# Gates of the last 64 dense tokens are read from the stage buffers instead of from DRAM

## The chip, the cores and the metric

One core of one Trainium2 chip runs the whole kernel. The metric is the device time of one execution in microseconds, given as the median of several runs. The engines are TensorE (PE; its weight loads are PEld), VectorE (DVE), ScalarE (ACT), GpSimd (POOL) and SyncE (SP), which here only issues transfers.

## What is computed

The kernel computes one encoder block on 512 tokens of width 1024: adaLN, two attention branches, a merged projection, and a PEER layer. Only the PEER layer matters here. It has 16384 experts, each one row of `expert_u` and one of `expert_v`; every token picks 16 experts in each of 8 heads, 128 in all, each with a gate.

```python
cand = (v1[..., :, None] + v2[..., None, :])      # scores of pairs of sub-keys
top, ci = lax.top_k(cand, PEER_TOPK)              # 16 experts a head
eidx = e1 * PEER_N_KEYS + e2                      # expert number, e1 and e2 below 128
gate = jax.nn.softmax(top, axis=-1)
act = jax.nn.gelu(jnp.einsum('td,thkd->thk', xc, expert_u[eidx]), approximate=False)
wts = gate * act
y = jnp.einsum('thk,thkd->td', wts, expert_v[eidx])
```

## The kernel before

The 512 tokens lie as four blocks of 128. Block 0 is done sparsely: for each of its 128 slots the chosen rows are gathered by GpSimd (`gather`, L1056), and VectorE makes a dot product (`dot`, L1062) or adds a weighted row to `acc` (`add`, L1071). These `jobs` are strewn over the rest of the kernel by `run_jobs`: `J0` = 48 of them in the gate stage, the others in the main loop.

Blocks 1 to 3, the 384 dense tokens, are done against all experts, 128 experts at a time. Expert group `e` (0 to 127) has three steps. First the activation: `gelu_s` (L872) multiplies `uT[e]` with all dense tokens in 24 matmuls and leaves 128 x 384 values `am`. For `e` below 96, `run_ahead` (L881) does this early and parks the result in DRAM (`gls`); for the others it is done inside the main loop. Second the product with the gates. Third the accumulation `y += (gated am)^T @ v[e]`, 18 matmuls of 128x512 (L1220), with the operands split into a high and a low half by `split` (L90: ScalarE makes the high half at L91, VectorE the low half at L92). `w4` loads a weight block into `raw` (L799) and gives the tiles for its halves, `whi` and `wlo`.

The gates come from a stage of their own (L1092 to L1150), which turns the sparse choice into a dense table of gates. For each dense block `slots` (L1021) gives expert numbers and gates. Then four tokens at a time VectorE builds one-hot tiles `oh` (L1125) and `og` (L1130), TensorE multiplies them into PSUM (`pg`, L1137), and ScalarE copies the result into `stage` (L1139). A `stage` tile holds 128 x 128 expert numbers by 32 tokens; there are two of them in turn. When 32 tokens (a group) are full, SyncE writes the tile to DRAM in four pieces, one for each quarter of the experts (`gd`, L1146). There are 12 groups, 96 copies and 48 writes.

The main loop (L1196 to L1223) reads the gates back. `stage_s` (L1161) loads, for every eighth expert group, a tile `gch` with the gates of eight expert groups and all 12 token groups (L1164, 1.5 MB), and the values `am`; it runs four expert groups ahead. The first expert groups in the order are 96 to 103. L1201 then multiplies `am` by `gch`, and ScalarE and VectorE split the product into `ah` and `al`. `py`, the accumulators, take the PSUM banks of the gate stage.

Each engine and each transfer queue works through its instructions in order; the order is chosen when the program is built, by a planner that estimates when each instruction could run, so that loads and jobs can stand earlier than in the text. Tiles of a closed pool give up their place; a tile that is put there waits, tile by tile, for the last use of what was there. The pool of the main loop (`lp`, L1158) is opened after those of the gate stage (`gt`) and of the selection (`sel`) are closed.

## Time and profile before

| what | us |
|---|---|
| runs | 2009.19, 2010.34, 2011.33 |
| median | 2010.34 |
| the profiled execution | 2011.68 |
| its span, first to last instruction | 2009.8 |
| TensorE busy in the span | 1873.7 |
| VectorE busy | 1593.2 |
| ScalarE busy | 842.7 |
| GpSimd busy | 698.0 |

[...] The gate stage's copies run from 938.7 to 1314.3 us of the span, the main loop from there to the end. An average over the span hides which engine sets the pace in which stage. So it is read together with views of single stretches: the timeline (instructions in order of time, with the idle time before each and what ended it), the chain of work that ended last, and busy times by stretch. Busy times of TensorE are those of pipelined instructions with modelled ends.

### The profile page before, as it was taken

Reading aid. Unit: us, or ns where it says so; the run is one execution under the profiler, and the core shown is the slowest. Engines: PE = TensorE matmul, PEld = TensorE weight load, DVE = VectorE, ACT = ScalarE, POOL = GpSimd, SP = SyncE. Lnnn points to the kernel's source line nnn. Section 1 sums busy time; section 2 is a strip of 40 time slices with the busy share of each in tenths; the row PEclk is TensorE's granted clock in tenths of the full one; section 3 lists DMA queues with packets and bytes.
Section 4 is the critical chain, followed back from the end, with each engine's and each line's share of the span. In section 5 each row is a group of like instructions: output and inputs, shape, how many; then the busy total and the mean of one; then the engine's idle time right before and its main releaser. Section 6 shows DMA issues by size and latency. Waiting matters only on the chain.

```text
span 2009.8 us, 28332 instructions
## 1 busy us (share of the span) xinstructions
PE 1873.7 (93%) x9858; PEld 1620.1 (81%) x9858; DVE 1593.2 (79%) x3276; ACT 842.7 (42%) x1330; POOL 698.0 (35%) x534
## 2 busy tenths in 40 slices
PE   6999998989899899999989999839999999999998
PEld 5987777778677788899989999828888888878886
DVE  7488585886775759999979989968778888888764
ACT  3444454645633333345545555513333333333342
POOL 2554332352235522012444147233234334323200
PEclk9999999999999999999999999969999999999999
DMA  7334242122256322468688979889999999999962
GB/s 262 86 120 121 63 145 60 35 87 84 59 152 215 128 72 81 147 226 276 229 295 316 322 274 322 299 287 371 360 320 354 342 354 330 355 361 325 345 225 93
DMA packets 206417, 447.30 MB, mean 223 GB/s; under 512 B 17297, under 2 KB 104642, under 8 KB 206146
## 3 DMA queue, kind: packets, MB, share of 16 engines
q1 hardware_dynamic: 168592, 309.14, 45.5%
q0 software_dynamic: 36864, 134.23, 18.8%
q10 hardware_dynamic: 818, 2.12, 0.3%
q8 instruction: 77, 1.26, 0.3%
q14 instruction: 66, 0.54, 0.1%
HBM read 397.20 MB, written 48.23 MB: 222 GB/s over the span
## 4 chain that ended last, share of the span: by engine, by line
PE 51%; DVE 16%; DMA 6%; issue 3%; ACT 2%; POOL 1%; SPq 0%; DVEq 0%; ACTq 0%; POOLq 0%
PE y L1220 26%; PE pj L86 7%; PE pj L87 7%; PE pj L88 7%; DMA raw<-uT 3%; DVE wlo L92 2%; DVE og L1130 2%; PE pg L1137 1%; DVE mr L933 1%; DMA raw<-w_ada 1%; DVE idx L935 1%; ACT whi L91 1%; DMA raw<-expert_v 1%; DVE oh L1125 1%; DVE idx L932 1%
## 5 line engine op out<-in xcount | busy, mean ns | idle before, releaser
L91 ACT ACTIVATE whi<-raw 128x1024 fp32r<-128x1024 f32 (+3 forms) x431 | 382.0, 893 | 382.6 <-PE pj L88 108.5
L92 DVE TENSOR_TENSOR wlo<-raw,whi 128x1024 fp32r<-128x1024 f32 (+3 forms) x339 | 376.9, 1114 | 98.1 <-ACT whi L91 96.7
L86 PE MATMUL pj<-h2h,whi 128*128 128x384 f32 x1008 | 345.8, 343 | 12.0 <-ACT am L879 10.9
L88 PE MATMUL pj<-h2h,wlo 128*128 128x384 f32 x1008 | 344.8, 342 | 5.0 <-DVE wlo L92 5.0
L87 PE MATMUL pj<-h2l,whi 128*128 128x384 f32 x1008 | 345.3, 343 | 0.0
L1058 POOL DMA_INDIRECT gat<-expert_v,eidx x128 | 211.9, 1656 | 316.9 <-DVE acc L1076 219.2
L1058 POOL DMA_INDIRECT gat<-expert_u,eidx x128 | 169.1, 1321 | 401.9 <-DVE gscr L1064 228.2
L1220 PE MATMUL y<-whi,ah 128*128 128x512 f32 x768 | 232.5, 397 | 33.3 <-ACT ah L91 28.4
L1220 PE MATMUL y<-wlo,ah 128*128 128x512 f32 x768 | 243.3, 397 | 0.7 <-DVE wlo L92 0.7
L92 POOL TENSOR_TENSOR wlo<-raw,whi 128x512 fp32r<-128x512 f32 (+2 forms) x92 | 146.5, 1598 | 278.7 <-ACT whi L91 256.0
L1220 PE MATMUL y<-whi,al 128*128 128x512 f32 x768 | 234.5, 395 | 0.0
L91 ACT ACTIVATE ah<-am 128x384 fp32r<-128x384 f32 x128 | 67.0, 524 | 333.5 <-PE y L1220 229.2
L86 PEld LDWEIGHTS pj<-h2h,whi 128*128 128x128 f32 x1008 | 192.2, 191 | 15.7 <-ACT am L879 12.9
L86 PE MATMUL pj<-whi,hh 128*128 128x512 f32 (+2 forms) x512 | 191.7, 387 | 9.8 <-DVE gA L651 4.4
L1220 PEld LDWEIGHTS y<-whi,ah 128*128 128x128 f32 x768 | 144.3, 189 | 67.7 <-ACT ah L91 28.6
L87 PE MATMUL pj<-wlo,hh 128*128 128x512 f32 (+2 forms) x512 | 196.2, 384 | 2.3 <-DVE wlo L92 2.3
L88 PEld LDWEIGHTS pj<-h2h,wlo 128*128 128x128 f32 x1008 | 191.9, 190 | 6.3 <-DVE wlo L92 6.3
L87 PEld LDWEIGHTS pj<-h2l,whi 128*128 128x128 f32 x1008 | 191.8, 190 | 1.1
L88 PE MATMUL pj<-whi,hl 128*128 128x512 f32 (+2 forms) x512 | 191.1, 380 | 0.0
L1220 PEld LDWEIGHTS y<-wlo,ah 128*128 128x128 f32 x768 | 144.7, 188 | 36.1 <-DVE wlo L92 1.2
L1220 PEld LDWEIGHTS y<-whi,al 128*128 128x128 f32 x768 | 144.2, 188 | 35.3
L1076 DVE SCALAR_TENSOR_TENSOR acc<-gat,wts,acc 128x1024 f32<-128x1024 f32 x127 | 162.4, 1279 | 9.6 <-DMA gat<-expert_v,eidx 9.2
(313 smaller groups left out, 3209.5 us busy)
## 6 DMA issues: line engine op xcount, KB each, us to landing
raw<-uT SPq DMA_DIRECT2D x128, 512.0 KB
raw<-expert_v SPq DMA_DIRECT2D x128, 512.0 KB
gd<-stage SPq DMA_DIRECT2D x48, 512.0 KB
gch<-gd SPq DMA_DIRECT2D x16, 1536.0 KB
raw<-w_in SPq DMA_DIRECT2D x88, 256.0 KB
am<-gls SPq DMA_DIRECT2D x96, 192.0 KB
gls<-am SPq DMA_DIRECT2D x94, 192.0 KB
raw<-w_ada SPq DMA_DIRECT2D x64, 256.0 KB
```

Source lines behind the costliest of these rows:

```text
L86: nc.tensor.matmul(ps, lh, rh, start=start, stop=False)
L87: nc.tensor.matmul(ps, lh, rl, start=False, stop=False)
L88: nc.tensor.matmul(ps, ll, rh, start=False, stop=stop)
L91: nc.scalar.activation(hi, raw, AF.Copy)
L92: (eng or nc.vector).tensor_tensor(lo, raw, hi.bitcast(F32), op=OP.subtract)
L932: nc.vector.max_index(out=i[:, 0:8], in_max=v[:, 0:8], in_values=s)
L933: nc.vector.match_replace(out=r, in_to_replace=v[:, 0:8], in_values=s, imm_value=-3.0e38)
L935: nc.vector.max_index(out=i[:, 8:16], in_max=v[:, 8:16], in_values=r)
L1058: nc.gpsimd.indirect_dma_start(out=t, out_offset=None, in_=src, in_offset=bass.IndirectOffsetOnAxis(ap=eidx[:, s:s + 1], axis=0))
L1076: nc.vector.scalar_tensor_tensor(acc, t, wts[:, s:s + 1], acc, op0=OP.mult, op1=OP.add)
L1130: nc.vector.tensor_tensor(o, oh[0].rearrange("p e t -> p t e"), gp[i][:, ts, None].to_broadcast([128, T, 128]), op=OP.mult)
L1220: nc.tensor.matmul(ys[b][n], l[:, bs], r[:, n * 512:n * 512 + 512], start=n_ == 0 and i == 0, stop=n_ == 127 and i == 2)
```

## The change

The two `stage` tiles become the two halves of one tile `stg` in the pool `g0`, which lives until the end of the kernel. Group `grp` (0 to 11) is built in half `grp % 2`, as before. Groups 0 to 9 are written to DRAM as before; groups 10 and 11 are not written, and their halves stay. The DRAM table and `gch` shrink from 12 to 10 token groups. The multiply by the gates becomes two: 320 values by `gch`, 64 values by `stg`. In the gate stage `slots` for block 0 now allocates its tiles ahead of `iota`.

```diff
-    RT, OB, SB, J0, GB = 8, 3, 2, 48, 4
+    RT, OB, J0, GB = 8, 3, 48, 4
...
+    stg = g0.tile([128, 2, 128, 32], F32, name="stage")
     gt = K.wk = Pool("gates")
...
+    e1, e2, g = slots(gt, 0)
     iota = gt.tile([128, 128, T], HF, name="iota")
     nc.vector.tensor_copy(iota, ioti[:, :, None].to_broadcast([128, 128, T]))
-    e1, e2, g = slots(gt, 0)
...
-            if tb == 0:
-                st = gt.tile([128, 128, 32], F32, name="stage", bufs=SB)
+            grp = 4 * b + t0 // 32
+            st = stg[:, grp % 2]
...
-            if tb == 28:
+            if tb == 28 and grp < 10:
                 for c in range(4):
-                    nc.sync.dma_start(gd[c][4 * b + t0 // 32].rearrange("c p e t -> p c (e t)"),
+                    nc.sync.dma_start(gd[c][grp].rearrange("c p e t -> p c (e t)"),
...
-            gch[e // 8] = lp.tile([128, 12, 8, 32], F32, name="gch", bufs=2)
+            gch[e // 8] = lp.tile([128, 10, 8, 32], F32, name="gch", bufs=2)
...
-        nc.vector.tensor_tensor(amv, amv, gch[e // 8][:, :, e % 8, :], op=OP.mult)
+        nc.vector.tensor_tensor(amv[:, :10], amv[:, :10], gch[e // 8][:, :, e % 8, :], op=OP.mult)
+        nc.vector.tensor_tensor(amv[:, 10:], amv[:, 10:], stg[:, :, e, :], op=OP.mult)
...
-        A['gd'] = [dram.tile([12, 4, 128, 8, 32], F32, name=f"gd{c}") for c in range(4)]
+        A['gd'] = [dram.tile([10, 4, 128, 8, 32], F32, name=f"gd{c}") for c in range(4)]
```

## Rows read from the trace of the kernel before

**Rows 1.** Page, first part: busy us, share of the span and instructions, each engine.
```profile
PE 1873.7 (93%) x9858; PEld 1620.1 (81%) x9858; DVE 1593.2 (79%) x3276; ACT 842.7 (42%) x1330; POOL 698.0 (35%) x534
```

**Rows 2.** Timeline, hand-over: start, us, engine, line, out<-in, count [idle before <-releaser].
```profile
1314.26 1.06 ACT L1139 ACTIVATE stage<-pg 128x512 f32<-128x512 f32 x1 [1.28 <-PE pg L1137]
...
1314.44 1.23 DVE L1064 SCALAR_TENSOR_TENSOR gscr<-gat,h2tok 128x1024 bf16<-128x1024 f32 x1
...
1315.35 3.82 SPq L1146 DMA_DIRECT2D gd<-stage  x4
...
1318.49 0.18 DVE L1069 TENSOR_TENSOR wts<-wts,gate 128x16 f32<-128x16 f32 x1 [0.28 <-ACT wts L1068]
...
1322.53 1.28 DVE L1076 SCALAR_TENSOR_TENSOR acc<-gat,wts,acc 128x1024 f32<-128x1024 f32 x1 [3.86 <-DMA gat<-expert_v,eidx]
...
1329.30 1.06 SPq L1164 DMA_DIRECT2D gch<-gd  x2
...
1341.39 1.96 DVE L1201 TENSOR_TENSOR am<-am,gch 128x384 f32<-128x384 f32 x4 [9.58 <-DMA gch<-gd]
...
1342.61 1.22 PE L1220 MATMUL y<-whi,ah 128*128 128x512 f32 x2 [28.38 <-ACT ah L91]
```

**Rows 3.** Chain that ended last, 1225 to 1372: start us, us, what.
```profile
1271.60 10.62 DMA raw<-uT
...
1317.40 11.76 DMA gd<-stage
1329.30 11.99 DMA gch<-gd
...
1357.24 4.20 PE y L1220 x18
```

**Rows 4.** Groups by line, 1342 to 2010: busy us, mean ns, idle before, releasers.
```profile
L1220 PE MATMUL y<-wlo,ah 128*128 128x512 f32 x768 | 243.3, 397 | 0.7 <-DVE wlo L92 0.7
...
L88 PE MATMUL pj<-h2h,wlo 128*128 128x384 f32 x208 | 71.3, 343 | 0.9 <-DVE wlo L92 0.9
...
L1201 DVE TENSOR_TENSOR am<-am,gch 128x384 f32<-128x384 f32 x127 | 69.6, 554 | 36.5 <-DMA am<-gls 27.2 <-ACT am L879 8.7
L91 ACT ACTIVATE ah<-am 128x384 fp32r<-128x384 f32 x128 | 67.0, 524 | 333.5 <-PE y L1220 229.2 <-issue 51.5 <-DVE am L1201 42.9
...
L1069 DVE TENSOR_TENSOR wts<-wts,gate 128x16 f32<-128x16 f32 x5 | 0.9, 178 | 0.6 <-ACT wts L1068 0.6
```

**Rows 5.** Busy by stretch: length; PE, PEld, DVE, ACT, POOL; PEclk, DMA share, GB/s.
```profile
1342.00:1366.00 24.00, 23.39 (x105) 20.45 (x106) 19.91 (x24) 8.51 (x13) 10.57 (x8) 0.91 0.69 233
...
1316.00:1342.00 26.00, 0.00 (x0) 0.00 (x0) 9.39 (x12) 0.22 (x1) 8.03 (x9) 0.50 1.02 358
1342.00:1900.00 558.00, 549.74 (x2489) 461.67 (x2490) 455.98 (x593) 192.24 (x265) 207.66 (x169) 0.99 0.95 343
1900.00:2003.00 103.00, 102.79 (x441) 82.38 (x439) 55.13 (x75) 34.45 (x46) 2.20 (x2) 1.00 0.53 171
```

**Rows 6.** Timeline of SyncE's queue, writes of the two groups before the last.
```profile
1262.53 3.21 SPq L1146 DMA_DIRECT2D gd<-stage  x4
...
1297.84 3.16 SPq L1146 DMA_DIRECT2D gd<-stage  x4
```

**Rows 7.** Groups by line and form, VectorE, whole span.
```profile
L952 DVE TENSOR_TENSOR cand<-vals 128x64 f32<-128x64 f32 x16 | 5.3, 334 | 0.0
```

**Rows 8.** Timeline, TensorE at the end of the gate stage.
```profile
1300.33 0.55 PE L1137 MATMUL pg<-og,oh 128*128 128x128 f16 x7 [0.35 <-DVE og L1130]
...
1303.00 0.91 PE L1137 MATMUL pg<-og,oh 128*128 128x128 f16 x7 [0.30 <-DVE og L1130]
```

**Rows 9.** One line, L1034: duration ns min/median/max, first and last start.
```profile
L1034 DVE TENSOR_TENSOR ef<-eq x4: 412/416/420, 883.5 to 1029.5; 128x256 f32<-128x256 bf16 x4
```

**Rows 10.** Timeline of the start: two pieces of one tile are read.
```profile
6.33 1.23 DVE L252 SCALAR_TENSOR_TENSOR sq<-xt 128x1024 bf16<-128x1024 f32 x1 [5.20 <-DMA xt<-x]
...
8.98 1.23 DVE L252 SCALAR_TENSOR_TENSOR sq<-xt 128x1024 bf16<-128x1024 f32 x1 [0.44 <-DMA xt<-x]
```

## The prediction

> **What bounds the kernel now.** I read the engine table of the page first: TensorE is busy for 93% of the span [rows 1], so the question is where it is not. The timeline of the hand-over from the gate stage to the main loop shows the largest hole after the start-up: TensorE stops when the last gate matmuls are done, and its first matmul of the main loop starts at 1342.61 after 28.38 us of idleness [rows 2]. The reader should follow that hole down the timeline. ScalarE copies the last four tokens' gates into `stage` at 1314.26 for 1.06 us. SyncE issues the four writes of the last group from 1315.35, and only at 1329.30 does it issue the first read back. VectorE's first multiply starts at 1341.39; ScalarE's split and TensorE at 1342.61 follow [rows 2]. The chain that ended last prices the two transfers: 11.76 us for the write that landed last and 11.99 us for the read [rows 3]. Together with the issue they are the hole; nothing else is late in it.

> The second question is whether time won there is kept until the end. The main loop after the hole is paced by TensorE. Its accumulations take 4.20 us for 18 matmuls, one expert after another [rows 3], and it is busy for 549.7 of 558 us and then for 102.8 of 103 [rows 5]: 8.5 us idle in the whole loop, 0.6 of them before its first matmul. So a loop that starts earlier ends earlier, as long as VectorE (456 of 558 us busy), the transfers (0.95 of the engines' time) and ScalarE (192 of 558) keep up [rows 5].

> **The change part by part.** *The round trip leaves the path.* The first chunk read will need only groups 0 to 9. Group 9 is the write issued at 1262.53, two before the last [rows 6]. With the last write's 11.76 us after 3.2 us of issue it has landed by about 1278, and a read like the present one (11.99 us) is in by about 1290, some 25 us before the last gates are copied at 1315.32. What must be free for it is the place of the `gch` buffer. By the code's sizes `sel` (6656 bytes a partition) and the `rb`, `sh`, `rkm`, `rkt` tiles of `slots` (3584) make 10240, exactly the new `gch`; the next 10240 are `eq` and `ef`. That the two pools start at the same address is my inference. The last use of `eq` and `ef` by VectorE begins at 1029.5 [rows 9], so both places would be long free; `iota`, which is read to the end, now lies behind them.

> *What is late next.* The multiply by groups 10 and 11 waits for the last copy, which ends at 1315.32. From the start of the first multiply to TensorE's start it is 1342.61 - 1341.39 = 1.22 us now [rows 2]; with a 64-wide multiply, about 0.33 us shorter, 0.89. The earliest start is thus 1316.2. But VectorE then has dot products of the sparse jobs, three from 1314.44 on, and a small product at 1318.49 behind them [rows 2]. They are queued work that goes on without the gates, and the multiply stands behind one to all of them: a start between 1316.6 and 1319.6. I take the middle, 1318.1, a gain of 1342.6 - 1318.1 = 24.5 us. The outer bound is a sum `acc` placed in front of it, which now ends at 1323.8 because it waits for its gather [rows 2]: start 1324.7, gain 17.9.

> *Clock.* [...] But the clock had fallen before the hole: seven gate matmuls take 0.55 us at 1300.33 and 0.91 at 1303.00, when TensorE runs only short bursts [rows 8]. [...]

> *One VectorE instruction more per expert.* The 384-wide multiply takes 554 ns, the 16-wide one of the same kind 178 [rows 4], so 1.02 ns an element: 320 wide 489, 64 wide 227. The sum of 716 is 162 ns more, 128 times, 21 us. The dearest row for 64 elements is the addition with repeated operands, 334 ns [rows 7]: then 269 ns more, 34 us. The cheap end is nothing, where VectorE was waiting anyway; a gain is excluded, since no element is saved. I take 21, as the 64-wide multiply is of the kind of [rows 4]. The work that hides it is VectorE's own waiting: 102 of 558 us while the jobs run, 48 of 103 after them [rows 5]. [...]

> *Jobs that move.* In the hole VectorE did 9.4 us of work and the transfer engines were full at 1.02 and 358 GB/s [rows 5]; those were 2.1 MB of gates out, 3.1 MB of gates in and eight gathers of 0.5 MB. The gathers and sums (9.4 us on VectorE) now fall into the loop. VectorE gets 21 + 9 = 30 us more against 102 us of waiting. The transfers get 4.2 MB more from the gathers and 3.7 MB less from 14 chunk reads that are 0.26 MB smaller: no change. TensorE's waits on VectorE are 0.9 + 0.7 = 1.6 us in the loop [rows 4]; I let them double: +1.6 us (0 to 8, where the end doubles the whole idle time of the loop).

> *SyncE's queue.* Eight writes fall away, 3.16 us of issue at 1297.84 and 3.82 at 1315.35 [rows 2, 6]; nothing on the path stood behind them. The two early reads are new ahead of loads in the gate stage. A read that waits at its place for group 9's write holds the loads of `raw` behind it: at most from 1265.7 to 1277.5, 11.8 us. I take 0, since the planner may put them anywhere up to 1300.

> *Sum.* The profiled execution took 2011.68 us, 1.9 outside its span: 2011.68 - 24.5 + 1.6 = 1988.8. The median of the runs is 1.34 below the profiled one: **1987.4 us**.

> **The rivals.** *The read is late all the same (0.08).* Some tile under `gch` lives to the end of the gate stage, or SyncE's order puts the read behind the last copy. Then it is issued at about 1315.4, lands 11.99 later and TensorE starts at 1328.6: only the write's half is won, 14 us, 1998. For it speaks that the place is my inference; against it that those tiles are done by 1030 [rows 9].

> *The gate stage pays (0.10).* The blocked queue just described delays a load of `raw`, and one such load at 1271.60, 10.62 us long, is on the chain that ended last [rows 3]. Up to 11.8 us come back: 1999. Any other re-planning of the gate stage has that size too; a part of it could eat most of the gain.

> *VectorE becomes the bound (0.08): slower.* Its place is the loop until the jobs end, where it is 82% busy. Its 30 us (43 with the 334 ns row) would all reach TensorE if VectorE's waits were forced by order and could not be filled. It decides from the point where more than 24.5 us get through; with all of 34 + 9 it is 2010.3 - 24.5 + 43 = 2029, with 30 it is 2016. Against it: TensorE waits 1.6 us for VectorE now, while ScalarE waits 229 us for TensorE with its split of `am` [rows 4].

> *The change is not what it says (0.04): slower.* The two stage buffers become halves of one tile. If a half's write had to wait for the other half's transfer, each of nine groups would stand for up to the 14 us from 1315.35 to 1329.30 [rows 2], 126 us; with half of it covered by the buffers ahead, 63 us are lost, 24.5 won, and it ends near 2049. It decides from 24.5 / 9 = 2.7 us a group. Against it: `xt` is one tile filled by four transfers, and a piece of it is read at 6.33 while another is still awaited at 8.98 [rows 10].

> **How the numbers follow.** Forecast 0.70, the others 0.08, 0.10, 0.08 and 0.04. The forecast's own range goes from 1979 (start at 1316.2, clock kept, and a few us from 4 MB less traffic in the gate stage) to 2001 (start at 1324.7 with 8 us of waits). The range 1979 to 2003 takes in the first two rivals' times and leaves out the slower two, part of the second, and little of the forecast. A difference under 0.2% (4 us) can't be told from no change. Faster: 0.70 + 0.08 + 0.07 of the second rival = 0.85; within 0.2%: 0.03 of it and 0.02 of the VectorE case; slower: 0.06 + 0.04 = 0.10.

> **What would show it.** Right: TensorE's idle time at the hand-over is 2 to 6 us with the last `stage` copy as its releaser; the first two `gch` reads are issued before 1300 and land before the last copy; the loop lasts 658 to 664 us from first to last accumulation; VectorE's busy time in it is 25 to 45 us higher, and waits of TensorE on `wlo` and `al` stay under 10 us. The late read would show as a first multiply released by the `gch` transfer; the blocked queue as a last copy later than 1318; VectorE's bound as TensorE waiting for `al` or `wlo` by 20 us or more; the shared tile as ScalarE's `stage` copies waiting for `gd` transfers. Wrong in size would be mostly the place of the multiply in VectorE's queue.

## The result, and the profile after

The changed kernel takes 1987.87 us (median of six runs, 1983.12 to 1992.97), the kernel before, run beside it, 2010.84 (six runs, 2006.71 to 2016.8). The ratio is 0.9883, with a 95% interval from 0.9864 to 0.9903: faster by 23 us. The forecast was 1987.4, in a range from 1979 to 2003. The profiled execution took 1988.12 us, 23.6 less than that of before.

First the page of the changed kernel: its span, and the busy time, share and instructions of each engine (before: [rows 1]).

```profile
span 1986.3 us, 28451 instructions
...
PE 1872.4 (94%) x9858; PEld 1618.9 (82%) x9858; DVE 1603.0 (81%) x3404; ACT 843.5 (42%) x1330; POOL 712.6 (36%) x534
```

TensorE does the same work in the same time. VectorE has 128 instructions more, and 9.8 us more busy time. So the 23 us are idle time of TensorE, and the hand-over is where to look. The timeline of the changed kernel answers to [rows 2] (start, us, engine, line, out<-in, count, and in brackets the idle time before and what ended it):

```profile
1302.71 1.12 SPq L1166 DMA_DIRECT2D gch<-gd  x2
...
1315.15 1.06 ACT L1141 ACTIVATE stage<-pg 128x512 f32<-128x512 f32 x1 [1.25 <-PE pg L1139]
...
1316.49 0.62 DVE L1204 TENSOR_TENSOR am<-am,stage 128x64 f32<-128x64 f32 x4
1317.03 1.21 DVE L1064 SCALAR_TENSOR_TENSOR gscr<-gat,h2tok 128x1024 bf16<-128x1024 f32 x1
...
1319.37 1.25 DVE L1064 SCALAR_TENSOR_TENSOR gscr<-gat,h2tok 128x1024 bf16<-128x1024 f32 x1 [1.12 <-DMA gat<-expert_u,eidx]
...
1320.91 0.20 DVE L1069 TENSOR_TENSOR wts<-wts,gate 128x16 f32<-128x16 f32 x1 [0.28 <-ACT wts L1068]
1321.03 1.68 DVE L1203 TENSOR_TENSOR am<-am,gch 128x320 f32<-128x320 f32 x4
1321.54 0.94 ACT L91 ACTIVATE ah<-am 128x384 fp32r<-128x384 f32 x2 [0.66 <-DVE am L1203]
...
1322.12 1.22 PE L1223 MATMUL y<-whi,ah 128*128 128x512 f32 x2 [7.00 <-ACT ah L91]
```

The last gates are copied at 1316.21, and TensorE goes on 5.9 us later; before, 27.3 us lay between 1315.32 and 1342.61. Its idle gap is 7.00 us instead of 28.38. The small multiply by the gates on chip runs as soon as they are there, at 1316.49. The wide one, by the gates from DRAM, comes last: VectorE does two more dot products of a sparse job first, waits 1.12 us for the gather of the second of them, and then does the small product that ScalarE's `wts` had held up.

In the kernel before, the read stood in SyncE's queue until the last write had landed (what waited for what: us in total, times, longest). The read of the changed kernel has no such wait.

```profile
SPq L1164 <- DMA gd<-stage: 10.0, 1, 10.0
```

The chain of work that ended last says the same (start, us, what; before: [rows 3]):

```profile
1313.22 6.06 DMA gat<-expert_u,eidx
1319.37 1.26 DVE gscr L1064 x2
1320.66 0.22 ACT wts L1068
1320.91 0.20 DVE wts L1069
1321.10 0.41 DVE am L1203
1321.54 0.53 ACT ah L91
1322.12 11.10 PE y L1223 x36
```

The write and the read of [rows 3] have left the chain. In their place stands a gather of a sparse job, which has nothing to do with the gates: it is only ahead in VectorE's queue.

The read itself is a surprise. SyncE issues it at 1302.71, behind three loads of `raw`, not before 1290; the view of that line has the time from issue to landing for one of the two reads that are issued there:

```profile
L1166 SPq DMA_DIRECT2D gch<-gd x2: 454/536/619, 1302.7 to 1303.2; - x2
...
DMA to landing us min/median/max: 14.8/14.8/14.8
```

The 14.8 us are those of the second read, which was issued at 1303.22, landed at 1318.0 and serves the next eight expert groups. The first one, which the multiply at 1321.03 waits for, had landed at 1313.3 by the trace's record of its semaphore, 10.6 us after its issue. That is 2.9 us before the last copy ends and 7.7 us ahead of the multiply, so the read costs nothing here, but the margin of 25 us before the last copy that the prediction gave it was not there.

After the hand-over: busy times by stretch (length; PE, PEld, DVE, ACT, POOL; granted clock, DMA share, GB/s; before: [rows 5]) and TensorE's waits once the loop has begun (what waited for what: us in total, times, longest).

```profile
1322.00:1346.00 24.00, 23.88 (x104) 20.77 (x105) 21.43 (x27) 7.83 (x13) 12.27 (x9) 0.89 0.76 272
1322.00:1880.00 558.00, 553.37 (x2502) 464.88 (x2503) 466.40 (x699) 193.81 (x267) 227.96 (x172) 0.99 0.95 342
1880.00:1983.00 103.00, 99.60 (x427) 79.77 (x425) 60.59 (x102) 32.18 (x43) 8.60 (x4) 1.00 0.55 181
```

```profile
PE y L1223 <- ACT whi L91: 2.8, 3, 1.4
PE pj L86 <- ACT whi L91: 1.1, 1, 1.1
PE pj L88 <- DVE wlo L92: 0.6, 1, 0.6
```

From first to last accumulation the loop takes 657.1 us, before 659.8; TensorE waits 2.8 + 1.1 + 0.6 = 4.5 us in it, before 7.6. The largest of these waits before was

```profile
PE y L1220 <- ACT whi L91: 4.9, 4, 1.5
```

That closes the account of the two profiled executions: the hand-over is 21.4 us shorter, the last copy came 0.9 later, the loop is 2.7 shorter and what lies behind the last accumulation 0.3: 23.5 of the 23.6 us.

### The profile page after: what moved, and what is told of

It is laid out like the page before. It is cut to its first block, busy times and chain, and to the rows that moved or that the text cites. A ratio compares the mean times of both kernels' runs of the same rounds, so it can differ in the third digit from the quotient of the medians.

```text
span 1986.3 us, 28451 instructions
## 1 busy us (share of the span) xinstructions
PE 1872.4 (94%) x9858; PEld 1618.9 (82%) x9858; DVE 1603.0 (81%) x3404; ACT 843.5 (42%) x1330; POOL 712.6 (36%) x534
## 4 chain that ended last, share of the span: by engine, by line
PE 49%; DVE 16%; issue 10%; POOL 4%; DMA 4%; ACT 2%; DVEq 0%; POOLq 0%; ACTq 0%; SPq 0%
PE y L1223 27%; PE pj L86 6%; PE pj L87 6%; PE pj L88 6%; POOL gat L1058 4%; DVE wlo L92 2%; DMA raw<-uT 1%; DMA gat<-expert_u,eidx 1%; DVE mr L933 1%; DMA raw<-w_ada 1%; DVE idx L935 1%; DVE idx L932 1%; DVE sm L605 1%; DVE og L1132 1%; DVE cand L952 1%
## 5 line engine op out<-in xcount | busy, mean ns | idle before, releaser
L1058 POOL DMA_INDIRECT gat<-expert_v,eidx x128 | 221.8, 1733 | 288.3 <-DVE acc L1076 196.9
```

The costliest lines, as they stand in the source:

```text
L1058: nc.gpsimd.indirect_dma_start(out=t, out_offset=None, in_=src, in_offset=bass.IndirectOffsetOnAxis(ap=eidx[:, s:s + 1], axis=0))
```

## The experiments

The theory at this point: TensorE's start was set by a wait for a write and a read of the last gates; without it, the start is set by the place of the multiplies in VectorE's queue, and the extra instruction per expert disappears in VectorE's waiting. Against it stood four others: that the extra instruction costs something which the gain hides; that the gain is the traffic saved and not the wait; that the late read is the next thing on the path, or that the order of the tiles (`slots` ahead of `iota`) decides when it is issued; and that the shorter loop comes from the smaller reads.

The write of group 9 is issued anywhere from 1256.0 to 1268.8 us in these executions, behind code that hardly differs. So this table compares each profiled execution by its own stretches: the hand-over, from the end of the last `stage` copy to the first accumulation of the loop, the loop, from the first to the last accumulation, and the gate stage's end, from the write of group 9 to that copy (us).

| kernel | hand-over | loop | group 9 to last copy | VectorE busy, span |
|---|---|---|---|---|
| before | 27.3 | 659.8 | 52.8 | 1593.2 |
| the change | 5.9 | 657.1 | 53.0 | 1603.0 |
| the change again | 5.2 | 657.1 | 53.9 | 1601.3 |
| split only, on the kernel before | 27.7 | 659.0 | 53.3 | 1602.8 |
| six multiplies | 6.4 | 656.9 | 54.7 | 1633.5 |
| last groups written all the same | 7.0 | 654.3 | 53.6 | 1602.8 |
| `iota` ahead of `slots` | 7.6 | 656.8 | 52.7 | 1600.1 |
| one group kept | 7.1 | 657.6 | 55.1 | 1604.9 |
| first gates in a tile of their own | 1.1 | 657.9 | 55.1 | 1601.4 |
| reads of the old size | 5.7 | 656.8 | 52.7 | 1600.5 |

Much of the spread of the hand-over among the changed kernels is one wait that has nothing to do with the gates, VectorE's wait for the gather of its last dot product. It is 1.12 us in the change, 2.23 with the last groups written, 2.45 with one group kept and 2.85 with `iota` ahead. Without it the hand-over is 4.7 to 4.8 us in all four.

**The split alone, on the kernel before.** All 12 groups go through DRAM as before; only the multiply is in two.

```diff
-        nc.vector.tensor_tensor(amv, amv, gch[e // 8][:, :, e % 8, :], op=OP.mult)
+        nc.vector.tensor_tensor(amv[:, :10], amv[:, :10], gch[e // 8][:, :10, e % 8, :], op=OP.mult)
+        nc.vector.tensor_tensor(amv[:, 10:], amv[:, 10:], gch[e // 8][:, 10:, e % 8, :], op=OP.mult)
```

> The kernel before, with only the multiply by the gates split into 320 and 64 values, both read from gch; all 12 groups still go through DRAM. Theory (VectorE's own waiting hides the second instruction): VectorE is busy 18 to 21 us longer in the main loop (484 + 218 ns against 554), TensorE's idle time in the loop after its first matmul stays under 10 us (7.6 in the kernel before), time within 4 us of before. Rival (VectorE is the bound in the loop): the 19 us reach TensorE, time 10 to 20 us above before.

It took 2012.25 us (ten runs, 2007.24 to 2019.01), a ratio of 1.0003 (0.9988 to 1.0018) to the kernel before. The timeline of this kernel shows the old hole:

```profile
1319.68 3.48 SPq L1146 DMA_DIRECT2D gd<-stage  x4
...
1333.43 1.06 SPq L1164 DMA_DIRECT2D gch<-gd  x2
...
1347.34 1.22 PE L1221 MATMUL y<-whi,ah 128*128 128x512 f32 x2 [28.79 <-ACT ah L91]
```

The extra 128 instructions cost nothing that can be measured (by the interval, between -2.4 and +3.6 us), and bring nothing either. What the change gained is therefore not in the split. VectorE's busy time grew by 9.6 us, and not by the expected 18 to 21.

**Six multiplies instead of two.** If the waiting of VectorE hides one instruction, how many does it hide? The 320 values are multiplied in five instructions of 64.

```diff
-        nc.vector.tensor_tensor(amv[:, :10], amv[:, :10], gch[e // 8][:, :, e % 8, :], op=OP.mult)
+        for h in range(0, 10, 2):
+            nc.vector.tensor_tensor(amv[:, h:h + 2], amv[:, h:h + 2], gch[e // 8][:, h:h + 2, e % 8, :], op=OP.mult)
```

> The change with the 320-wide multiply cut into five of 64, so that each expert has six multiplies of 218 ns instead of 484 + 218: 0.61 us more an expert, 78 us more on VectorE, against some 90 us of its waiting while the jobs run and 42 after them. Theory (waiting hides it until it is used up): TensorE's idle time in the loop grows by less than 25 us, time 1988 to 2013, VectorE over 95% busy while the jobs run, which end later. Rival (each us on VectorE reaches TensorE, so that the change already paid some 20 us): time 2060 to 2070.

1987.84 us (four runs, 1980.17 to 1995.82), ratio 0.9874 (0.9844 to 0.9904): the same as the change. First the two multiplies of the change, in its groups by line (busy us, mean ns of one, idle before and its releasers), then their counterparts in this kernel, and a stretch of its loop (columns as above).

```profile
L1203 DVE TENSOR_TENSOR am<-am,gch 128x320 f32<-128x320 f32 x128 | 62.0, 486 | 22.4 <-DMA am<-gls 12.5 <-ACT am L879 9.7
...
L1204 DVE TENSOR_TENSOR am<-am,stage 128x64 f32<-128x64 f32 x128 | 27.6, 218 | 0.0
```

```profile
L1204 DVE TENSOR_TENSOR am<-am,gch 128x64 f32<-128x64 f32 x640 | 97.6, 217 | 27.7 <-DMA am<-gls 21.5 <-ACT am L879 5.9
...
L1205 DVE TENSOR_TENSOR am<-am,stage 128x64 f32<-128x64 f32 x128 | 27.4, 216 | 0.0
```

```profile
1330.00:1888.00 558.00, 552.23 (x2504) 463.17 (x2505) 490.02 (x1113) 192.39 (x266) 246.70 (x172) 1.00 0.95 340
```

512 more instructions than in the change make VectorE busy for 30.5 us more of the span (1633.5 against 1603.0, in the table), and for 490 of 558 us here, 88%. The loop still takes 656.9 us. This load was expected to be 78 us; it is less than half, because each instruction of 217 ns begins before the one ahead has ended: 640 of them are busy for 97.6 us, 152 ns each. The case in which VectorE becomes the bound is thus farther away than its rival in the prediction had it.

**The last two groups are written all the same, and not read.** This puts the traffic back and leaves the wait away.

```diff
-            if tb == 28 and grp < 10:
+            if tb == 28:
...
-                              gd[e // 32][:, e // 8 % 4].rearrange("h p e t -> p h (e t)"))
+                              gd[e // 32][0:10, e // 8 % 4].rearrange("h p e t -> p h (e t)"))
```

> The change, but groups 10 and 11 are still written to DRAM in eight writes, as before; nobody reads them, and their gates are taken from the stage halves. Theory (what the change removes is the wait of the read for the last write, not the traffic): the first read is issued before the last write, hand-over from the end of the last stage copy to TensorE 5.5 to 7.5 us, loop 656 to 658 us, time as with the change, 1986 to 1992. Rival (the 4.2 MB of writes at the end of the gate stage are part of the price): the read lands later beside the last write, hand-over 10 to 14 us, time 1993 to 1998.

1990.72 us (four runs, 1982.24 to 1991.3), ratio 0.9899 (0.987 to 0.9928). Its timeline:

```profile
1301.65 2.91 SPq L1148 DMA_DIRECT2D gd<-stage  x4
...
1307.35 6.01 SPq L1166 DMA_DIRECT2D gch<-gd  x2
...
1320.69 3.89 SPq L1148 DMA_DIRECT2D gd<-stage  x4
...
1327.66 1.22 PE L1223 MATMUL y<-whi,ah 128*128 128x512 f32 x2 [8.09 <-ACT ah L91]
```

The last write is issued as soon as the last copy has ended, at 1319.60 + 1.06 = 1320.66, as in the kernel before, and nothing of the hand-over waits for it: the hand-over is 7.0 us. The loop, 654.3 us, is shorter than expected. So the gain is the wait for the last write and the read behind it, not the eight writes and their bytes.

**`iota` ahead of `slots`, as before.** The prediction derived from sizes that the first `gch` lies where tiles of `slots` were, so that it is free early. Here `iota` is put in that place; it is read until the gate stage ends.

```diff
-    e1, e2, g = slots(gt, 0)
     iota = gt.tile([128, 128, T], HF, name="iota")
     nc.vector.tensor_copy(iota, ioti[:, :, None].to_broadcast([128, 128, T]))
+    e1, e2, g = slots(gt, 0)
```

> The change with iota allocated ahead of the slots tiles again, so that the first gch lies over iota, which VectorE reads until the last one-hot. Theory (the place under gch matters): the first read is issued after the last one-hot, at about 1311 instead of 1302.7, lands some 12 to 15 us later, TensorE starts its main loop at 1325 to 1330 instead of 1322.1, time 1991 to 1996. Rival (the place does not matter, the queue order sets the read): issue near 1303, start at 1322, time as with the change, 1988.

1990.95 us (four runs, 1985.52 to 1991.79), ratio 0.9892 (0.9862 to 0.9921). SyncE's waits (from 1250 to 1345) and the timeline of this kernel:

```profile
SPq L1166 <- DVE oh L1127: 8.0, 1, 8.0
```

```profile
1312.02 1.04 SPq L1166 DMA_DIRECT2D gch<-gd  x2
...
1317.88 0.63 DVE L1204 TENSOR_TENSOR am<-am,stage 128x64 f32<-128x64 f32 x4
...
1322.50 1.23 DVE L1064 SCALAR_TENSOR_TENSOR gscr<-gat,h2tok 128x1024 bf16<-128x1024 f32 x1 [2.85 <-DMA gat<-expert_u,eidx]
...
1324.13 1.68 DVE L1203 TENSOR_TENSOR am<-am,gch 128x320 f32<-128x320 f32 x4
...
1325.22 1.22 PE L1223 MATMUL y<-whi,ah 128*128 128x512 f32 x2 [8.71 <-ACT ah L91]
```

Now the read waits 8.0 us for VectorE's `oh`, which reads `iota`, and is issued only 5.6 us before the last copy ends, instead of 13.5 as in the change. The inference about the place is borne out. But the hand-over is 7.6 us, against 5.2 and 5.9 in the two executions of the change, and the time cannot be told from theirs: the multiply at 1324.13 has no wait for `gch` ahead of it. So its read had landed by then, at most 12.1 us after the issue at 1312.02. What grew is the wait for the gather, 2.85 us; whether the later read slows that gather is not shown. VectorE's queue is late enough to hide even this read, so the order of the tiles is worth about 2 us at most.

**Only the last group kept on chip.** Group 10 goes through DRAM too; `iota` moves to the pool that lives to the end, so that the larger `gch` still finds a free place.

```diff
-    iota = gt.tile([128, 128, T], HF, name="iota")
+    iota = g0.tile([128, 128, T], HF, name="iota")
...
-            if tb == 28 and grp < 10:
+            if tb == 28 and grp < 11:
...
+        nc.vector.tensor_tensor(amv[:, :11], amv[:, :11], gch[e // 8][:, :, e % 8, :], op=OP.mult)
+        nc.vector.tensor_tensor(amv[:, 11:], amv[:, 11:], stg[:, 1:, e, :], op=OP.mult)
```

> The change with only the last group (32 tokens) kept on chip; group 10 is written and read with the other ten (gch with 11 groups, 352 and 32 values; iota lies in g0 so that it is not under gch). Theory (the round trip of the last group that goes through DRAM sets the start as soon as it ends after the gate stage): group 10 is written at about 1298 and lands by 1305 to 1310, the first read follows and lands at 1320 to 1325, TensorE starts at 1323 to 1328, time 1989 to 1994. Rival (each group kept is worth half of what the change gives, because transfers are what counts): time 1998 to 2001. Rival (one group is enough, the read's own start was set by SyncE's queue and not by the write): start at 1322, time 1988.

1987.79 us (four runs, 1981.52 to 1993.49), ratio 0.9887 (0.9849 to 0.9925). SyncE's waits and the timeline:

```profile
SPq L1166 <- DMA gd<-stage: 4.1, 1, 4.1
SPq L1166 <- DVE oh L1127: 3.0, 1, 3.0
```

```profile
1302.03 3.83 SPq L1166 DMA_DIRECT2D gch<-gd  x2
...
1310.00 1.07 ACT L1141 ACTIVATE stage<-pg 128x512 f32<-128x512 f32 x1 [1.27 <-PE pg L1139]
...
1318.18 1.22 PE L1223 MATMUL y<-whi,ah 128*128 128x512 f32 x2 [8.21 <-ACT ah L91]
```

I had expected a start from 1323 to 1328 from the wait for group 10's write. That write was on its way from 1290.55; the two reads waited 4.1 us for it and 3.0 us for `oh`, and were issued between 1302.03 and 1305.86, still 5 us before the last copy ended at 1311.07. One group on chip buys as much as two here: what matters is that the write of the last group is not waited for.

**The first gates in a tile of their own.** If only VectorE's queue is left, then gates that arrive long before must let the wide multiplies of the first four experts run early. A tile of 5 KB a partition takes the gates of groups 0 to 9 for these experts and is read right behind group 9's write.

```diff
+    early = g0.tile([128, 10, 4, 32], F32, name="early")
...
+                if grp == 9:
+                    nc.sync.dma_start(early.rearrange("p h e t -> p h (e t)"),
+                                      gd[NS // 32][:, NS // 8 % 4, :, 0:4, :].rearrange("h p e t -> p h (e t)"))
...
+        gs = early[:, :, e - NS, :] if NS <= e < NS + 4 else gch[e // 8][:, :, e % 8, :]
+        nc.vector.tensor_tensor(amv[:, :10], amv[:, :10], gs, op=OP.mult)
```

> The change, plus a tile of 5 KB a partition in the long-lived pool that is filled, right behind group 9's writes, with the gates of the first four experts of the loop (groups 0 to 9); their 320-wide multiplies read it. Theory (what is late now is the place of the 320-wide multiply in VectorE's queue, behind five dot products and a small product, because the planner starts the read only after the gate stage): the four multiplies move into the gate stage, the 64-wide ones are last, TensorE starts 2 to 3 us after the end of the last stage copy instead of 5.9; time 3 to 4 us below the change. Rival (the multiplies and the early read cost the gate stage what they win): hand-over 2 to 3 us, but the last copy comes 2 to 4 us later, time as with the change.

1990.26 us (six runs, 1979.49 to 1993.48), ratio 0.9886 (0.986 to 0.9913): no different from the change. The timeline:

```profile
1279.11 0.37 SPq L1152 DMA_DIRECT2D early<-gd  x1
...
1322.11 1.06 ACT L1142 ACTIVATE stage<-pg 128x512 f32<-128x512 f32 x1 [1.26 <-PE pg L1140]
...
1323.44 0.63 DVE L1209 TENSOR_TENSOR am<-am,stage 128x64 f32<-128x64 f32 x4
...
1324.28 1.22 PE L1228 MATMUL y<-whi,ah 128*128 128x512 f32 x2 [2.20 <-ACT ah L91]
```

The mechanism does what it should: the early read lands 9.6 us after its issue, the four wide multiplies start in the gate stage, from 1291.3 to 1299.8, and TensorE starts 1.1 us after the last copy, with 2.20 us of idleness. The 4 to 5 us so won in the hand-over don't reach the time: the gate stage's end takes 55.1 us instead of 53.0 to 53.9, and the loop 657.9. The wide multiplies and the early read now lie in the gate stage's end, but the kernel with one group kept has neither and takes 55.1 us there too, so that they cost it is not shown. By the sum of the three stretches 2 us should be left of the gain; that is within what executions differ by, and where the gain goes stays open.

**The change again**, as a measure of how far two executions of one program differ.

> The change itself once more, beside the other kernels of this call: 0.986 to 0.990 of the kernel before, hand-over from the end of the last stage copy to TensorE's first accumulation 5.5 to 6.5 us, loop 656 to 658 us.

1988.49 us (six runs, 1983.74 to 1991.74), ratio 0.9887 (0.9865 to 0.991), hand-over 5.2 (a little under the expected range) and loop 657.1: within 0.7 us of the first in both.

**Reads of the old size.** Each of the later chunk reads gets back the 0.26 MB that it lost, into a tile that nobody reads.

```diff
+            if len(gch) > 2:
+                gx = g0.tile([128, 2, 8, 32], F32, name="gx", bufs=2)
+                nc.sync.dma_start(gx.rearrange("p h e t -> p h (e t)"),
+                                  gd[e // 32][0:2, e // 8 % 4].rearrange("h p e t -> p h (e t)"))
```

> The change, but each of the 14 chunk reads inside the main loop is followed by a second read of two more groups (0.26 MB) into a tile that nobody uses, so that the loop moves as many bytes in as before. Theory A (the loop is 3 us shorter than before, 657.1 instead of 660.2 us from first to last matmul, because its transfers shrank): TensorE's idle time in the loop goes from 4.5 back to 7 to 8 us, time 1990 to 1992. Theory B (the bytes do not matter at this size; the 3 us are the re-planned order and the transfers that already were in place): idle time stays at 4 to 5 us, time 1988.

1990.15 us (four runs, 1988.57 to 1991.73), ratio 0.9894 (0.9867 to 0.9921). The loop takes 656.8 us, and TensorE waits 5.1 us in it. The bytes are back and the loop is as short as without them. So the smaller reads are not why the loop is 1 to 5 us shorter in the changed kernels than in the two that read all 12 groups back. The first read is issued only at 1311.86 in this kernel, 9 us later than in the change, and the hand-over is no longer for it: one more sign that the read is not on the path.

## Why the prediction was right, point by point

**The round trip leaves the path: right, with a wrong time for the read.** The write and the read back are gone from the chain, and the runs with the split alone and with the writes put back leave only the wait as the cause. But "in by about 1290" failed by 23 us: the first read landed at 1313.3. The place of `gch` was free, and group 9's data had landed by 1273.7, at most 8.6 us after the issue of a piece; the read stands behind loads of `raw` in SyncE's queue, and the last three of them are issued from 1293.24 to 1302.66, one by one as buffers of `raw` come free: the second at 1297.45 and the third at 1302.33, each 0.03 us after a `wlo` of VectorE has ended (1297.42 and 1302.30). The prediction weighed where the read could be, and not behind what the planner had put it. The rival of the late read still did not come true: the first read was issued 13.5 us before the last copy ended and not after it, and landed 2.9 us before that. Only the second read landed after the copy, at 1318.0, and nothing waited for it.

**What is late next: right in kind, short by 4 us.** VectorE's queue is next, as forecast. The term was 1318.1, 2.8 us after the last copy; measured are 5.9, and TensorE is idle for 7.0 us, not for 2 to 6. The forecast took the 64-wide multiply as the last one to be ready and put it behind one to all of the queued products. It was the 320-wide one that stood last, behind all of them and a wait of 1.12 us for a gather. The gain there is 21.4 us instead of 24.5; the outer bound, 1324.7, held. The run with the first gates in a tile of their own confirms the mechanism: with the wide multiplies out of the way the hand-over is 1.1 us.

**Clock: left out of the sum, rightly.** The granted clock of the loop's first 24 us is 0.89, not higher than the 0.91 of [rows 5]. In the change the granted clock is at half (0.50 of full speed) from the first matmul of the loop until 1327.52, for 5.4 us; before, it was 3.9 us, from 1342.61 to 1346.47. At half clock the matmuls of 512 columns start in pairs 0.85 us apart; behind that the pairs are 0.47 us apart. The cost is about half of each stretch, 2.7 and 1.9 us, estimated from the share of 0.50. No run shows the "clock kept" at the fast end of the forecast's range: even after a gap of 2.20 us, in the run with the early tile, the pairs start 0.85 us apart for the first 5.3 us (1324.28 to 1329.56). By the same measure it is 5.3 us in the change and 3.6 before. As the prediction had read it, the clock had fallen ahead of the gap: it was at half from 1300.21 on in the change, from 1302.10 on before, when TensorE ran only bursts of at most eight gate matmuls and 1.24 us. The other kernels differ as much at one length of gap: the slow pace lasts 5.3 us after a gap of 6.34 us (the change again), and 2.7 us both after 8.09 (last groups written) and after 28.79 (the split alone).

**One VectorE instruction more: hidden, and the term was twice too large.** Busy times of the groups add up to 62.0 + 27.6 = 89.6 us against 70.1, and 19.5 more looks like the 21 of the forecast. But VectorE's busy time over the whole span grew by only 9.8 us (9.6 with the split alone), since the small multiply begins before the wide one has ended and the next instruction before the small one has. Two stretches of VectorE's timeline in the loop show it, of the change first, then of the kernel before:

```profile
1401.95 0.49 DVE L1203 TENSOR_TENSOR am<-am,gch 128x320 f32<-128x320 f32 x1 [0.80 <-DMA am<-gls]
1402.36 0.22 DVE L1204 TENSOR_TENSOR am<-am,stage 128x64 f32<-128x64 f32 x1
1402.50 1.22 DVE L92 TENSOR_TENSOR wlo<-raw,whi 128x1024 fp32r<-128x1024 f32 x1
```

```profile
1404.06 0.55 DVE L1201 TENSOR_TENSOR am<-am,gch 128x384 f32<-128x384 f32 x1
1404.53 1.23 DVE L92 TENSOR_TENSOR wlo<-raw,whi 128x1024 fp32r<-128x1024 f32 x1
```

From the start of the multiplies to that of `wlo` it takes 0.55 us with two of them, 0.47 with one. That is 0.08 us an expert, 10 us in all. Each instruction starts about 0.08 us before the one ahead has ended, the small one as well as the wide one, so this split pays less than the sum of durations says. That the instruction is hidden was right: six multiplies cost no more than two.

**Jobs that move: right in kind, 6.4 us instead of 9.4.** VectorE's busy time in the loop is 466.4 + 60.6 - 456.0 - 55.1 = 15.9 us higher: 9.8 of the split and 6.4 of five sums `acc` that fell into the hole before (96 in the loop instead of 91). The forecast named 25 to 45. Most of what it missed by is the mis-sized split; the rest is that its 9.4 us for the hole took in dot products and a small product, which in the changed kernel still run before the loop.

**The loop: the sign was wrong.** It should have become 1.6 us longer and is 2.7 shorter. TensorE's waits are 4.5 us instead of 7.6. The term priced only the waits on VectorE, 1.6 us, and let them double; they fell to 0.6. The larger part of what went is a wait that it left out, of TensorE for ScalarE's `whi`, 4.9 us before and 2.8 now. That is not a matter of the split (8.8 us of waits with it alone) nor of the bytes. What remains common to the kernels with a short loop is the earlier start, and so other times of the sparse jobs against the experts. No run tells this apart from the planner's new order, and the cause stays open.

**SyncE's queue and the gate stage: right.** From group 9's write to the last copy it took 53.0 us, before 52.8, and the two halves of one tile did not make ScalarE's copies wait for `gd` transfers: all their waits from 938 to 1317, 64.1 us, ended with TensorE's `pg`. With that the blocked queue and the tile that is waited for as a whole are out. VectorE as the bound is out by TensorE's waits: 0.6 us for `wlo`, none for `al`.

**The sum.** 3.1 us too much gain in the hand-over, a last copy 0.9 later, and 4.3 us too little gain in the loop: errors of opposite sign, which brought the forecast to 0.5 us of the median (and that of the profiled execution, 1988.8, to 0.7 us of the measured 1988.12). The part that was right is the hole and what would take its place; the closeness is luck.

## What to carry to other kernels

When a transfer there and back is taken off the path, price what is next in the queue of each engine that it ran through: here the wide multiply started 7.7 us after its gates had landed, behind queued work that has nothing to do with the data, down to a wait of 1.12 us for a gather of another job. Look too at which loads the planner has placed ahead of a new pool's first read; that its place is free and its data is there (by 1273.7 here) doesn't bring it forward (1302.71). And small instructions more on an engine that waits anyway can be free: here even five more for each expert were, with VectorE busy for 88% of the time while the jobs run. Where that ends no run shows.
